# RMSNorm with swish on one core: one queue for x, and blocks of 8 rows instead of 4

## The chip, the cores and the metric

The kernel runs on one core of a Trainium2 chip. The metric is the device time of one execution in microseconds (us), the median over several runs. A profile is of one execution; its span is the time from the first to the last instruction that the profiler recorded.

Engines: DVE is VectorE, ACT is ScalarE, POOL is GpSimd, SP is SyncE (which here only issues transfers and waits). DMA means the core's 16 transfer engines. ACTq and SPq are the sequencers of ACT and SP, where transfers are issued. TensorE does nothing here.

## The reference

```python
batch, seq, dim = 16, 1024, 512          # x: float32, gamma: ones, eps: 1e-5

def reference(x, gamma, eps):
    rms = np.sqrt(np.mean(x ** 2, axis=-1, keepdims=True) + eps)
    x_norm = x / rms * gamma
    return (x_norm * (1.0 / (1.0 + np.exp(-x_norm)))).astype(np.float32)
```

x has 16384 rows of 512 floats, 33.55 MB; the output has the same size. So 67.1 MB must be moved. A row's result needs the sum of its squares, then `(mean + eps) ** -0.5`, a multiplication by this number and by gamma, and swish.

## The kernel before

Each of the 128 partitions owns 128 rows of x. They are cut into four groups of 32 rows per partition ("32 rows" always means 32 rows in each partition, 8.4 MB). The buffer `xb` holds 96 rows per partition: groups 0, 1 and 2 have places of their own, group 3 takes the place of group 0 (`slots`). Everything is done in place in `xb`, and the order of every engine's work is written out by hand with semaphores.

- Loads (`load`, L117) are issued by SP in the order of the list `loads`: 4, 4, 8, 16 and 32 rows of groups 0 and 1, then 28 + 4 rows of group 2 and 28 + 4 of group 3. Two are issued before the program's first barrier (`early`). A load whose place is still to be stored waits on SP for that store's landing (`st`).
- Stores (`store`, L191) are issued by ACT, in the middle of its stream of work: 28 + 4 rows of group 0, groups 1 and 2 whole, then 16 + 8 + 8 rows of group 3. Two of them are held back until a given load has landed (`hold`, L189), so that a store doesn't share the transfer engines with a load.
- Compute goes in chunks of `cn = 4` rows, 32 chunks. For chunk k, ACT squares: two rows go one at a time through an `activation` whose accumulator writes the row's mean of squares (L162, output to a `junk` tile), two rows are squared into a PSUM tile `sq` (L169), and DVE sums these (`sums`, L215). GpSimd adds eps (L143) and raises to the power -0.5 (L150). DVE multiplies each row by the result and gamma, one instruction a row (`norm`, L226). ACT applies swish to the 4 rows at once (`swish`, L181).
- The order on ACT is: squares of chunk k, stores that are due, swish of chunk k-2. The order on DVE is: sums of chunk k, multiplications of chunk k-1.
- At the start GpSimd clears three small tiles (L137 to L139), ACT loads gamma into four partitions (L199) and DVE spreads it (L239).

Of the kernel before, what the change touches and what calls it, by code (L numbers as in the profile page):

```python
# [9 lines left out]
def kernel(  # L10
# [7 lines left out]
    nc = tc.nc  # L18
    P = nc.NUM_PARTITIONS
    AF = mybir.ActivationFunctionType  # L20
    ALU = mybir.AluOpType
    fp32 = mybir.dt.float32

    xf = x.flatten_outer_dims()
    of = out.flatten_outer_dims()
    R, D = xf.shape

    groups = [32] * 4
    slots = [0, 32, 64, 0]
    loads = [(0, 0, 4), (0, 4, 4), (0, 8, 8), (0, 16, 16), (1, 0, 32)]  # L30
    loads += [(2, 0, 28), (2, 28, 4), (3, 0, 28), (3, 28, 4)]
    stores = [(0, 0, 28), (0, 28, 4), (1, 0, 32), (2, 0, 32)]
    stores += [(3, 0, 16), (3, 16, 8), (3, 24, 8)]
    hold = {0: (loads.index((2, 0, 28)), 12), 2: (loads.index((3, 0, 28)), 22)}
    behind = {}
    ring = 96
    early = 2
    cn = 4
    n_sq = 2

    first = [sum(groups[:g]) for g in range(len(groups))]
    assert P * sum(groups) == R, R
# [1 line left out]

    chunks = []
    for i, (g, r, n) in enumerate(loads):
        for c in range(r, r + n, cn):
            chunks.append((slots[g] + c, i if c == r else None))
    K = len(chunks)
    assert K * cn * P == R  # L50

    ends = [-(-(first[g] + r + n) // cn) for g, r, n in stores]

    inv_d = 1.0 / float(D)
    eps_f = float(eps)
# [4 lines left out]
    def sbuf(name, shape, dt=fp32):  # L60
        return nc.alloc_sbuf_tensor(name, shape, dt).ap()

    xb = sbuf("xb", [P, ring, D])
    gamma4 = sbuf("gamma4", [P, D])
    gamma_sb = sbuf("gamma_sb", [P, D])
    neg_half = sbuf("neg_half", [P, cn])
    ms = sbuf("ms", [P, K, cn])
    aeps = sbuf("aeps", [P, K, cn])
    rstd = sbuf("rstd", [P, K, cn])
    sq = [nc.alloc_psum_tensor(f"sq{i}", [P, n_sq, D], fp32).ap() for i in range(2)]  # L70
    junk = [nc.alloc_psum_tensor(f"junk{i}", [P, D], fp32).ap() for i in range(2)]

    ld = [nc.alloc_semaphore(f"ld{t}") for t in range(len(loads))]
    st = [nc.alloc_semaphore(f"st{t}") for t in range(len(stores))]
    scratch = nc.dram_tensor("scratch", [P, 16], fp32, kind="Internal").ap()
    blank = sbuf("blank", [P, 16])
    s_blank = nc.alloc_semaphore("s_blank")
    s_scratch = nc.alloc_semaphore("s_scratch")
    s_gld = nc.alloc_semaphore("s_gld")
    s_zero = nc.alloc_semaphore("s_zero")  # L80
    s_half = nc.alloc_semaphore("s_half")
    s_gamma = nc.alloc_semaphore("s_gamma")
    s_acc = nc.alloc_semaphore("s_acc")
    s_sq = nc.alloc_semaphore("s_sq")
    s_sum = nc.alloc_semaphore("s_sum")
    s_eps = nc.alloc_semaphore("s_eps")
    s_rstd = nc.alloc_semaphore("s_rstd")
    s_norm = nc.alloc_semaphore("s_norm")
    s_swish = nc.alloc_semaphore("s_swish")

    def need(ins, sem, value):
        return ins.wait_op(sem, value, "sem-ge")

    def dram(ap, piece):
        g, r, n = piece
        rows = ap[P * first[g] : P * (first[g] + groups[g])]
        return rows.rearrange("(p n) d -> p n d", n=groups[g])[:, r : r + n, :]

    def place(piece):
        g, r, n = piece  # L100
        return slots[g] + r, slots[g] + r + n

    def buf(piece):
        a, b = place(piece)
        return xb[:, a:b, :]

    stored_by_sync = set()

    def load(i):
        a, b = place(loads[i])  # L110
        for u, piece in enumerate(stores):
            c, d = place(piece)
            over = piece[0] < loads[i][0] and c < b and a < d
            if (over or behind.get(i) == u) and u not in stored_by_sync:
                nc.sync.wait_ge(st[u], 16)
                stored_by_sync.add(u)
        return nc.sync.dma_start(  # L117
            out=buf(loads[i]), in_=dram(xf, loads[i])
        ).then_inc(ld[i], 16)
# [3 lines left out]
    for t in range(early):  # L123
        ins = load(t).ins
        assert here[-1] is ins or here[-1].name == ins.name
        here.pop()
        at = next(
            i for i, other in enumerate(entry)
            if other.engine == mybir.EngineType.SP
            and isinstance(other, mybir.InstDrain)  # L130
        )
        entry.insert(at, ins)
    for t in range(early, len(loads)):
        load(t)
    nc.sync.wait_ge(s_scratch, 16)

    nc.gpsimd.memset(blank, 0.0).then_inc(s_blank, 1)  # L137
    nc.gpsimd.memset(gamma4, 0.0).then_inc(s_zero, 1)  # L138
    nc.gpsimd.memset(neg_half, -0.5).then_inc(s_half, 1)  # L139
    nc.gpsimd.wait_ge(s_half, 1)  # L140
    for k in range(K):
        need(
            nc.gpsimd.tensor_scalar(  # L143
                out=aeps[:, k, :], in0=ms[:, k, :], scalar1=eps_f, scalar2=None,
                op0=ALU.add,
            ),
            s_sum, k + 1,
        ).then_inc(s_eps, 1)
        need(
            nc.gpsimd.tensor_tensor(  # L150
                out=rstd[:, k, :], in0=aeps[:, k, :], in1=neg_half, op=ALU.pow
            ),
            s_eps, k + 1,
        ).then_inc(s_rstd, 1)

    def square(k):
        at, landing = chunks[k]
        if landing is not None:
            nc.scalar.wait_ge(ld[landing], 16)  # L159
        for j in range(n_sq, cn):  # L160
            n = k * (cn - n_sq) + j - n_sq
            acc = nc.scalar.activation(  # L162
                out=junk[n % 2], in_=xb[:, at + j, :], func=AF.Square,
                scale=inv_d**0.5, accum_out=ms[:, k, j : j + 1],
            )
            if n >= 2:
                need(acc, s_acc, n - 1)
            acc.then_inc(s_acc, 1)
        square = nc.scalar.activation(  # L169
            out=sq[k % 2], in_=xb[:, at : at + n_sq, :],  # L170
            func=AF.Square, scale=inv_d**0.5,
        )
        if k >= 2:
            need(square, s_sum, k - 1)
        square.then_inc(s_sq, 1)

    def swish(k):
        at, _ = chunks[k]
        rows = xb[:, at : at + cn, :]
        need(  # L180
            nc.scalar.activation(out=rows, in_=rows, func=AF.Silu), s_norm, k + 1  # L181
        ).then_inc(s_swish, 1)

    def after(t):
        return max((k for u, (_, k) in hold.items() if u <= t), default=0)

    def store(t):
        if t in hold:
            nc.scalar.wait_ge(ld[hold[t][0]], 16)  # L189
        need(  # L190
            nc.scalar.dma_start(out=dram(of, stores[t]), in_=buf(stores[t])),  # L191
            s_swish, ends[t],
        ).then_inc(st[t], 16)

    need(nc.scalar.dma_start(out=scratch, in_=blank), s_blank, 1).then_inc(
        s_scratch, 16
# [3 lines left out]
        s_zero, 1,  # L200
    ).then_inc(s_gld, 16)
    nc.scalar.preload_act_table_set("silu_and_others")  # L202
    stored = 0
    for k in range(K + 3):
        if k < K:
            square(k)
        while stored < len(stores) and max(ends[stored] + 2, after(stored)) <= k:
            store(stored)
            stored += 1
        if 2 <= k < K + 2:  # L210
            swish(k - 2)

    def sums(k):
        need(
            nc.vector.tensor_reduce(  # L215
                out=ms[:, k, 0:n_sq], in_=sq[k % 2], op=ALU.add,
                axis=mybir.AxisListType.X,
            ),
            s_sq, k + 1,
        ).then_inc(s_sum, 1)  # L220

    def norm(k):
        at, _ = chunks[k]
        for j in range(cn):
            row = xb[:, at + j, :]
            ins = nc.vector.scalar_tensor_tensor(  # L226
                out=row, in0=row, scalar=rstd[:, k, j : j + 1], in1=gamma_sb,
                op0=ALU.mult, op1=ALU.mult,
            )
            if j == 0:  # L230
                need(ins, s_rstd, k + 1)
        ins.then_inc(s_norm, 1)

    for k in range(K + 1):
        if k < K:
            sums(k)
        if k == 0:
            need(
                nc.vector.stream_shuffle(gamma_sb, gamma4, [0] * 32), s_gld, 16  # L239
            ).then_inc(s_gamma, 1)  # L240
        if k == 1:
            nc.vector.wait_ge(s_gamma, 1)
        if k >= 1:
            norm(k - 1)

    for t in range(len(stores)):
        if t not in stored_by_sync:
            nc.sync.wait_ge(st[t], 16)


# [33 lines left out]
```

## Time and profile before

| what | value |
|---|---|
| time, median of 3 runs | 161.33 us (159.96 to 161.42) |
| the profiled execution | 161.41 us, span 160.1 us |
| ACT busy | 129.7 us (81% of the span) |
| DVE busy | 124.4 us (78%) |
| POOL busy | 65.5 us (41%) |
| moved | 67.16 MB, mean 419 GB/s over the span |
| loads' queue (q1), stores' queue (q10) | 49.4% and 48.8% of the 16 transfer engines' time |

A row of the page's groups reads: line, engine, operation, output and inputs with their shapes, count, then the busy time in us and the mean of one in ns, then the idle time before them and what ended it. A row of the windows reads: stretch, its length, busy time of DVE, ACT and POOL in it (with counts), TensorE's clock, the mean busy share of the transfer engines, and GB/s. The share can be above 1 in a short stretch, since a packet is counted where it starts. The chain of waits is followed back from the last instruction of an engine; its pieces are given as start, length, and what was done.

### The profile page before, as it was taken

Reading aid. Unit: us, or ns where it says so; the run is one execution under the profiler, and the core shown is the slowest. Engines: PE = TensorE matmul, PEld = TensorE weight load, DVE = VectorE, ACT = ScalarE, POOL = GpSimd, SP = SyncE. Lnnn points to the kernel's source line nnn. Section 1 sums busy time; section 2 is a strip of 40 time slices with the busy share of each in tenths; the row PEclk is TensorE's granted clock in tenths of the full one; section 3 lists DMA queues with packets and bytes.
Section 4 is the critical chain, followed back from the end, with each engine's and each line's share of the span. In section 5 each row is a group of like instructions: output and inputs, shape, how many; then the busy total and the mean of one; then the engine's idle time right before and its main releaser. Section 6 shows DMA issues by size and latency. Waiting matters only on the chain.

```text
span 160.1 us, 496 instructions
## 1 busy us (share of the span) xinstructions
DVE 124.4 (78%) x162; ACT 129.7 (81%) x193; POOL 65.5 (41%) x71
## 2 busy tenths in 40 slices
DVE  0239989999199998899999999999999999970000
ACT  0937989994799988999999999999999999571000
POOL 1035555555055555555555555555555555500000
DMA  7999996996999997999969996996996997899896
GB/s 264 458 461 393 450 598 262 524 524 262 458 461 446 444 411 338 458 458 458 450 258 458 458 458 266 518 524 278 508 508 297 508 475 327 385 426 483 368 426 270
DMA packets 2460, 67.16 MB, mean 419 GB/s; under 512 B 404, under 2 KB 404, under 8 KB 408
## 3 DMA queue, kind: packets, MB, share of 16 engines
q1 hardware_dynamic: 1296, 33.56, 49.4%
q10 hardware_dynamic: 1160, 33.57, 48.8%
q14 instruction: 4, 0.03, 0.0%
HBM read 33.56 MB, written 33.56 MB: 419 GB/s over the span
## 4 chain that ended last, share of the span: by engine, by line
ACT 55%; DMA 24%; DVE 7%; issue 3%; ACTq 1%; SPq 0%
ACT xb L181 24%; DMA xb<-in_x_dram 24%; ACT junk L162 18%; ACT sq L169 13%; DVE xb L226 5%; DVE ms L215 2%; ACTq L191 1%; SPq L117 0%; ACTq L159 0%
## 5 line engine op out<-in xcount | busy, mean ns | idle before, releaser
L226 DVE SCALAR_TENSOR_TENSOR xb<-xb,rstd,gamma_sb 128x512 f32<-128x512 f32 x128 | 87.3, 744 | 0.0
L181 ACT ACTIVATE xb<-xb 128x2048 f32<-128x2048 f32 x32 | 60.9, 1902 | 4.8 <-DVE xb L226 3.8
L215 DVE TENSOR_REDUCE ms<-sq 128x2 f32<-128x1024 f32 x32 | 39.2, 1223 | 16.1 <-ACT sq L169 13.1
L143 POOL TENSOR_SCALAR aeps<-ms 128x4 f32<-128x4 f32 x32 | 20.6, 644 | 70.0 <-DVE ms L215 70.0
L150 POOL TENSOR_TENSOR rstd<-aeps,neg_half 128x4 f32<-128x4 f32 x32 | 44.0, 1376 | 2.7
L162 ACT ACTIVATE junk<-xb 128x512 f32<-128x512 f32 x64 | 37.2, 582 | 6.7 <-DMA xb<-in_x_dram 6.6
L169 ACT ACTIVATE sq<-xb 128x1024 f32<-128x1024 f32 x32 | 32.1, 1005 | 0.0
L162 ACT ACTIVATION_READ_ACCUMULATOR junk<-xb 128x1 f32 x64 | 11.9, 186 | 0.0
L202 ACT ACT_TABLE_LOAD x1 | 1.3, 1283 | 3.6 <-issue 3.6
L239 DVE LOAD_MASK_SELECT gamma_sb<-gamma x1 | 0.0, 14 | 2.5 <-DMA gamma<-in_gamma_dram 2.5
L239 DVE STREAM_SHUFFLE gamma_sb<-gamma 128x512 f32<-128x512 f32 x1 | 0.7, 715 | 0.0
L137 POOL MEMSET blank<- 128x16 f32 x1 | 0.1, 111 | 1.5 <-POOLq L58 1.5
L138 POOL MEMSET gamma<- 128x512 f32 x1 | 0.5, 525 | 0.0
L265 POOL MEMSET const-float32-0.0<- 128x1 f32 x1 | 0.1, 98 | 0.2 <-issue 0.2
L265 POOL MEMSET const-bfloat16-1.0<- 128x1 bf16 x1 | 0.1, 102 | 0.0
L265 POOL MEMSET const-uint8-127<- 128x1 uint8 x1 | 0.1, 101 | 0.0
L139 POOL MEMSET neg_half<- 128x4 f32 x1 | 0.1, 101 | 0.0
L265 POOL MEMSET const-float32-1.0<- 128x1 f32 x1 | 0.1, 98 | 0.0
## 6 DMA issues: line engine op xcount, KB each, us to landing
xb<-in_x_dram SPq DMA_DIRECT2D x2, 7168.0 KB, 38.4
out_dram<-xb ACTq DMA_DIRECT2D x1, 7168.0 KB, 19.3
xb<-in_x_dram SPq DMA_DIRECT2D x4, 1024.0 KB, 14.0
xb<-in_x_dram SPq DMA_DIRECT2D x1, 4096.0 KB, 19.5
out_dram<-xb ACTq DMA_DIRECT2D x1, 4096.0 KB, 20.1
out_dram<-xb ACTq DMA_DIRECT2D x2, 2048.0 KB, 16.1
xb<-in_x_dram SPq DMA_DIRECT2D x1, 2048.0 KB, 10.2
out_dram<-xb ACTq DMA_DIRECT2D x1, 1024.0 KB, 21.3
```

The source lines that it names most:

```text
L138: nc.gpsimd.memset(gamma4, 0.0).then_inc(s_zero, 1)
L143: nc.gpsimd.tensor_scalar(out=aeps[:, k, :], in0=ms[:, k, :], scalar1=eps_f, scalar2=None, op0=ALU.add,),
L150: nc.gpsimd.tensor_tensor(out=rstd[:, k, :], in0=aeps[:, k, :], in1=neg_half, op=ALU.pow),
L162: acc = nc.scalar.activation(out=junk[n % 2], in_=xb[:, at + j, :], func=AF.Square, scale=inv_d**0.5, accum_out=ms[:, k, j : j + 1],)
L169: square = nc.scalar.activation(out=sq[k % 2], in_=xb[:, at : at + n_sq, :], func=AF.Square, scale=inv_d**0.5,)
L181: nc.scalar.activation(out=rows, in_=rows, func=AF.Silu), s_norm, k + 1
L191: nc.scalar.dma_start(out=dram(of, stores[t]), in_=buf(stores[t])),
L202: nc.scalar.preload_act_table_set("silu_and_others")
L215: nc.vector.tensor_reduce(out=ms[:, k, 0:n_sq], in_=sq[k % 2], op=ALU.add, axis=mybir.AxisListType.X,),
L226: ins = nc.vector.scalar_tensor_tensor(out=row, in0=row, scalar=rstd[:, k, j : j + 1], in1=gamma_sb, op0=ALU.mult, op1=ALU.mult,)
L239: nc.vector.stream_shuffle(gamma_sb, gamma4, [0] * 32), s_gld, 16
L265: nc = _bacc.Bacc("TRN2", target_bir_lowering=False, num_devices=1)
```

## The change

SP issues the loads and the stores of x, all on its one queue, in a list `order`: loads of 8, 8, 16, 32 and 32 rows; stores of 24 and 8 rows of group 0; loads of 24 and 8 rows of group 3; then all other stores (groups 1 and 2, then 16 + 8 + 8 rows). A store waits on SP until swish has reached its last row. The holds are gone.

Compute goes in 16 blocks of 8 rows. Of these, 3 go through ACT's accumulator and 5 are squared into `sq` and summed by DVE. `sq` has two buffers of five rows; the first is in PSUM, the second now in SBUF. The addition of eps moves from GpSimd to DVE, right behind the sums, for all 8 rows; GpSimd does only the power, 16 times on 8 values instead of 32 times on 4. The three memsets move from GpSimd to DVE. Swish is one instruction for 8 rows, still two blocks behind the squares.

```diff
-    loads = [(0, 0, 4), (0, 4, 4), (0, 8, 8), (0, 16, 16), (1, 0, 32)]
-    loads += [(2, 0, 28), (2, 28, 4), (3, 0, 28), (3, 28, 4)]
-    stores = [(0, 0, 28), (0, 28, 4), (1, 0, 32), (2, 0, 32)]
+    loads = [(0, 0, 8), (0, 8, 8), (0, 16, 16), (1, 0, 32)]
+    loads += [(2, 0, 32), (3, 0, 24), (3, 24, 8)]
+    stores = [(0, 0, 24), (0, 24, 8), (1, 0, 32), (2, 0, 32)]
     stores += [(3, 0, 16), (3, 16, 8), (3, 24, 8)]
-    hold = {0: (loads.index((2, 0, 28)), 12), 2: (loads.index((3, 0, 28)), 22)}
+    turns = [(len(loads) - 2, 2)]
-    cn = 4
-    n_sq = 2
+    cn = 8
+    n_sq = {8: 5}
+    order = [("load", t) for t in range(early, turns[0][0])]
+    at = 0
+    for (i, u), (j, _) in zip(turns, turns[1:] + [(len(loads), 0)]):
+        order += [("store", t) for t in range(at, u)] + [("load", t) for t in range(i, j)]
+        at = u
+    order += [("store", t) for t in range(at, len(stores))]
...
-    sq = [nc.alloc_psum_tensor(f"sq{i}", [P, n_sq, D], fp32).ap() for i in range(2)]
+    sq = [
+        nc.alloc_psum_tensor("sq0", [P, n_max, D], fp32).ap(),
+        sbuf("sq1", [P, n_max, D]),
+    ]
...
-    for t in range(early, len(loads)):
-        load(t)
+    for kind, t in order:
+        if kind == "load":
+            load(t)
+        else:
+            need(
+                nc.sync.dma_start(out=dram(of, stores[t]), in_=buf(stores[t])),
+                s_swish, ends[t],
+            ).then_inc(st[t], 16)
...
-    nc.gpsimd.memset(blank, 0.0).then_inc(s_blank, 1)
-    nc.gpsimd.memset(gamma4, 0.0).then_inc(s_zero, 1)
-    nc.gpsimd.memset(neg_half, -0.5).then_inc(s_half, 1)
-    nc.gpsimd.wait_ge(s_half, 1)
-    for k in range(K):
-        need(
-            nc.gpsimd.tensor_scalar(
-                out=aeps[:, k, :], in0=ms[:, k, :], scalar1=eps_f, scalar2=None,
-                op0=ALU.add,
-            ),
-            s_sum, k + 1,
-        ).then_inc(s_eps, 1)
+    for k, (_, row, n, _) in enumerate(chunks):
         need(
             nc.gpsimd.tensor_tensor(
-                out=rstd[:, k, :], in0=aeps[:, k, :], in1=neg_half, op=ALU.pow
+                out=rstd[:, row : row + n], in0=ms[:, row : row + n],
+                in1=neg_half[:, :n], op=ALU.pow,
             ),
             s_eps, k + 1,
         ).then_inc(s_rstd, 1)
...
-    for k in range(K + 3):
+    for k in range(K + 2):
         if k < K:
             square(k)
-        while stored < len(stores) and max(ends[stored] + 2, after(stored)) <= k:
-            store(stored)
-            stored += 1
-        if 2 <= k < K + 2:
+        if k >= 2:
             swish(k - 2)
 
+    nc.vector.memset(blank, 0.0).then_inc(s_blank, 1)
+    nc.vector.memset(gamma4, 0.0).then_inc(s_zero, 1)
+    nc.vector.memset(neg_half, -0.5)
+
     def sums(k):
+        _, row, n, _ = chunks[k]
         need(
             nc.vector.tensor_reduce(
-                out=ms[:, k, 0:n_sq], in_=sq[k % 2], op=ALU.add,
-                axis=mybir.AxisListType.X,
+                out=ms[:, row : row + n_sq[n]], in_=sq[k % 2][:, : n_sq[n], :],
+                op=ALU.add, axis=mybir.AxisListType.X,
             ),
             s_sq, k + 1,
         ).then_inc(s_sum, 1)
+        need(
+            nc.vector.tensor_scalar(
+                out=ms[:, row : row + n], in0=ms[:, row : row + n],
+                scalar1=eps_f, scalar2=None, op0=ALU.add,
+            ),
+            s_sum, k + 1,
+        ).then_inc(s_eps, 1)
```

## The prediction

> **What bounds the kernel now.** I read the page first: engines, queues and chain.
>
> ```profile
> DVE 124.4 (78%) x162; ACT 129.7 (81%) x193; POOL 65.5 (41%) x71
> q1 hardware_dynamic: 1296, 33.56, 49.4%
> q10 hardware_dynamic: 1160, 33.57, 48.8%
> ACT 55%; DMA 24%; DVE 7%; issue 3%; ACTq 1%; SPq 0%
> ```
>
> The two transfer queues together fill 98.2% of the 16 transfer engines' time. The chain names ACT, but it is followed back from the last store, so it shows only why that store was issued when it was. The windows and the last store's landing (the view of `out_dram`, from 143 us on) show what ends the run:
>
> ```profile
> 145.00:160.00 15.00, 0.00 (x0) 0.00 (x0) 0.00 (x0) 1.00 0.91 387
> L191 ACTq DMA_DIRECT2D out_dram<-xb x1: 339/339/339, 144.9 to 144.9; - x1
> DMA to landing us min/median/max: 15.2/15.2/15.2
> ```
>
> All engines are done at 144.9 us, and the stores queued behind each other take 15 us more. Now the two 32-row stores before them, same view, other windows:
>
> ```profile
> L191 ACTq DMA_DIRECT2D out_dram<-xb x1: 338/338/338, 99.6 to 99.6; - x1
> DMA to landing us min/median/max: 21.8/21.8/21.8
> ...
> L191 ACTq DMA_DIRECT2D out_dram<-xb x1: 339/339/339, 114.3 to 114.3; - x1
> DMA to landing us min/median/max: 26.4/26.4/26.4
> ```
>
> Group 1's store lands at 99.6 + 21.8 = 121.4 and group 2's at 114.3 + 26.4 = 140.7, 19.3 us later. The other three land at 150.3, 155.2 and 160.1. So 32 rows cost 19.3 us of transfer, 16 rows 9.65, 8 rows 4.85, and everything after group 1's store takes 38.7 us. Group 2's store was issued 7.1 us before group 1's had landed. That lead is the number to watch: the transfers bound the kernel, compute is second, and its slack at that place is about 7 us, at the end 10 us (144.9 against 155.2).
>
> The compute pace, first from the page's groups:
>
> ```profile
> L226 DVE SCALAR_TENSOR_TENSOR xb<-xb,rstd,gamma_sb 128x512 f32<-128x512 f32 x128 | 87.3, 744 | 0.0
> L181 ACT ACTIVATE xb<-xb 128x2048 f32<-128x2048 f32 x32 | 60.9, 1902 | 4.8 <-DVE xb L226 3.8
> L215 DVE TENSOR_REDUCE ms<-sq 128x2 f32<-128x1024 f32 x32 | 39.2, 1223 | 16.1 <-ACT sq L169 13.1
> L143 POOL TENSOR_SCALAR aeps<-ms 128x4 f32<-128x4 f32 x32 | 20.6, 644 | 70.0 <-DVE ms L215 70.0
> L150 POOL TENSOR_TENSOR rstd<-aeps,neg_half 128x4 f32<-128x4 f32 x32 | 44.0, 1376 | 2.7
> L162 ACT ACTIVATE junk<-xb 128x512 f32<-128x512 f32 x64 | 37.2, 582 | 6.7 <-DMA xb<-in_x_dram 6.6
> L169 ACT ACTIVATE sq<-xb 128x1024 f32<-128x1024 f32 x32 | 32.1, 1005 | 0.0
> ```
>
> And two rows of the timeline, a stretch without waits on DVE (start, length, instruction):
>
> ```profile
> 136.40 1.23 DVE L215 TENSOR_REDUCE ms<-sq 128x2 f32<-128x1024 f32 x1
> 137.54 5.38 DVE L226 SCALAR_TENSOR_TENSOR xb<-xb,rstd,gamma_sb 128x512 f32<-128x512 f32 x8
> ```
>
> Eight multiplies take 5.38, so one every (5.38 - 0.744) / 7 = 0.662 us; the one behind a reduce starts 1.14 after it, 0.09 before its end. Back to back, DVE needs 2 x 1.14 + 8 x 0.662 = 7.58 us for 8 rows. ACT, in the chain, repeats 1.23 + 0.91 + 1.87 = 4.01 for 4 rows, 8.02 for 8. ACT sets the pace, with DVE close behind.
>
> **The change, part by part.**
>
> *Rows shift from ACT to DVE.* A block of 8 rows has 3 rows summed by ACT's accumulator and 5 by DVE's reduce; before it was 4 and 4.
> ACT per block: 3 accumulates at 1.23 / 2 = 0.615 give 1.84. The five-row square: one more 512 elements costs 1.005 - 0.581 = 0.424, so 1.005 + 3 x 0.424 = 2.28 (bounds 2.28 and, in proportion, 2.51). The eight-row swish: 1.90 + 4 x 0.424 = 3.60 (at most 3.80). Sum 7.7, less some 0.1 of overlap: ACT gains 0.4.
> DVE per block: the reduce of five rows isn't in the trace. A further row costs at least (1223 - 744) ns = 0.48 (reduce less a one-row multiply) and at most 1223 / 2 = 0.61. So it takes 2.66 to 3.06. The shuffle, like the reduce a one-source pass, is the nearest row: 715 ns for 512 elements, so 0.51 a row. I take 0.52 and 2.78. The add of eps on DVE is new. Lower bound nothing (hidden), upper 0.66 (GpSimd's median for this operation); I take a multiply without its elements, 0.744 - 0.53, about 0.20. It waits for its own reduce's semaphore: 0.04, as between a square's end and its reduce's start. Sum: 2.78 + 0.04 + 0.20 - 0.08 overlap + 8 x 0.662 = **8.24 us per block** (bounds 7.88 and 8.98). DVE becomes the bound, slower per row than ACT was.
>
> A rule that speaks against this change: the Trainium skill, page "VectorE: DVE Perf Modes", section "The perf-mode tier table (the rule you actually need)", gives `tensor_reduce` only the single-rate mode, in SBUF as in PSUM, so the SBUF half of the square buffer brings no rate. With the page's 0.96 GHz clock (section "Specifications") a row is 512 / 0.96 = 533 ns, an estimate from the page; the reduce would take 2.82, the block 8.28, and the end come 0.4 us later.
>
> *Blocks of 8 instead of 4.* Swish still comes two blocks behind the squares, so it trails by 16 rows instead of 8. At about 1 us a row this makes every store ready some 8 us later; it was 7.1 us early.
>
> *All of x on SP's queue.* ACT loses seven issues (0.34 to 1.05 us each; 1.0 us of idle before a swish at 60.5 is theirs). ACT no longer bounds, so this brings nothing. Order of SP: 96 rows of loads, stores of 24 and 8 rows, loads of 24 and 8, then the rest. Store 0 waits for swish 2 (about 49 us) and store 1 for swish 3 (about 57), both before the loads have landed. The load of 24 rows waits for store 0's landing; store 1, 4.85 us long, covers its start. In the kernel before, the last 32 rows of loads ran from store 1's landing at 80.7 to 101.9, 21.2 us instead of 19.3, so the fixed order saves 1.9. Transfers alone: 61.3 (the last load of the first 96 rows, issued at 3.9 and 57.4 under way) + 14.5 + 4.85 + 14.5 + 4.85 + 19.3 = 119.3 for group 1's store, + 38.7 = 158.0.
>
> *Covered edits.* GpSimd loses 32 adds and half the powers; DVE waits for a power only if it exceeds the eight multiplies between (5.3 us against 1.38; if uncovered, 1.4 per block). The memsets go to DVE, which idled until 7.2; gamma landed at 10.9 and is needed near 19. Without cover: 0.6 once.
>
> **The path that sets the end.** The load of group 1 lands at 41.14 as before (same bytes ahead of it):
>
> ```profile
> 2.75 38.38 DMA xb<-in_x_dram
> ```
>
> ACT begins at 41.22; block 4's squares take 1.84 + 2.28, and its reduce starts at 45.38. DVE is free by then: block 1's reduce starts at about 16.3 (load at 12.1, squares 4.1), three blocks of 8.24 and one wait of 1.4 for block 2's squares give 42.5. From 45.38 DVE runs without a pause, since ACT needs 7.6. Block 13's reduce starts at 45.38 + 9 x 8.24 = 119.5, which is when block 11's multiplies end (119.6). Swish 11: 3.60, to 123.2. Store 3 (group 2) is issued at 123.3, but SP's queue has been empty since 119.3. **That is the new wait.** A transfer into an idle queue: the first load, issued at 0.0, moves nothing for about 1.0 (the window 0 to 2 us has a share of 0.49), and its 4 rows land at 4.6, 2.2 more than their 2.4 of transfer. So 1.0 to 2.2; I take 1.2, since the start of the program burdens the larger one. End: 123.3 + 1.2 + 38.7 = 163.2. What follows has slack: store 4 is ready at about 140 (needed 144), store 5 at 148 (154), store 6 at 153.5 (158).
>
> The profiled execution took 161.41 with a span of 160.1, so 1.3 lie around it; the median of the runs is 161.33, 0.1 less. 163.2 + 1.3 - 0.1 = **164.4 us**, 1.9% above before.
>
> **Rivals.**
> A, faster: the queue never runs empty and the end is 158.0, 159.2 us in all. Store 3 must be issued by 119.3 - 1.2 = 118.1, so 9 blocks must fit in 118.1 - 3.7 - 45.4 = 69.0: 7.67 a block. For it: transfers fill 98% of the span. Against it: eight multiplies leave 2.4 for reduce and add, below even the lower bound of 2.66 for the reduce less its 0.08.
> B, no change: reduce at its lower bound, the add nearly hidden. 7.88 to 8.05 a block moves the end by 9 x (-0.36 to -0.19): 161.2 to 162.7.
> C, slower still: the add on DVE is as dear as on GpSimd. 0.66 instead of 0.20 makes the block 8.70, store 3 4.1 us later: 168.5. For it: GpSimd's median is 0.66. Against it: the shortest one there, at 8.5 us while DVE was idle, took 0.23, so 0.66 is not the price of the add itself.
>
> A second rule against the change stands by itself: the Trainium skill, "SBUF — State Buffer", section "Who interferes with whom", lets a two-port instruction such as the add wait until a GpSimd instruction has finished. No row of this trace has a blocked one; a whole power (1.38) would be 12 us over nine blocks, but the last power began a block's multiplies earlier and is over.
>
> **Numbers.** Forecast 0.66, A 0.12, B 0.14, C 0.08. Its own range is 163.1 to 166.3 (block 8.1 to 8.45). Left out may be A (0.12) and most of C (0.07), so the range takes in B and the lower edge of C: 161.2 to 167.2. About 1% can be told from no change here; so faster 0.12, same 0.14, slower 0.74.
>
> **What would show it.** DVE without idle time from about 45 to 150 us, ACT waiting for DVE before each swish; a block period of 8.1 to 8.45; store 3 issued near 123 and the transfer share near nothing for some 5 us from 119; the loads all landed near 100 instead of 102; the last multiplies near 150, the last swish near 153.5. If the reduce of five rows takes under 2.4 or the transfers run without a hole, the forecast is wrong.

## The result, and the profile after

The changed kernel takes 165.04 us (median of 4 runs, 164.93 to 165.18), against 160.82 us for the kernel before in the runs beside it (159.96 to 161.42). The ratio is 1.0267, 95% interval 1.0209 to 1.0324: slower, as forecast, at 164.4 us in a range of 161.2 to 167.2. The profiled execution took 164.93 us with a span of 163.6, so again 1.3 us lie around the span.

The page of the changed kernel (engines, loads' and stores' queue in one, and the chain):

```profile
DVE 132.8 (81%) x165; ACT 124.2 (76%) x129; POOL 32.9 (20%) x20
q1 hardware_dynamic: 2016, 67.11, 96.3%
DVE 64%; DMA 24%; ACT 5%; issue 0%; SPq 0%; ACTq 0%
```

ACT and DVE have changed places: DVE is now the busier engine, and the chain runs over DVE where it ran over ACT. All 67.11 MB went through one queue, at 96.3% of the transfer engines' span instead of 98.2%. The groups, with the rows that the forecast had to estimate:

```profile
L240 DVE SCALAR_TENSOR_TENSOR xb<-xb,rstd,gamma_sb 128x512 f32<-128x512 f32 x128 | 86.1, 746 | 0.0
L198 ACT ACTIVATE xb<-xb 128x4096 f32<-128x4096 f32 x16 | 57.8, 3615 | 13.5 <-DVE xb L240 13.5
L222 DVE TENSOR_REDUCE ms<-sq 128x5 f32<-128x2560 f32 x16 | 45.1, 2819 | 14.2 <-ACT sq L186 14.2
L163 POOL TENSOR_TENSOR rstd<-ms,neg_half 128x8 f32<-128x8 f32 x16 | 32.7, 2044 | 108.0 <-DVE ms L229 108.0
L186 ACT ACTIVATE sq<-xb 128x2560 f32<-128x2560 f32 x16 | 36.9, 2304 | 0.0
L229 DVE TENSOR_SCALAR ms<-ms 128x8 f32<-128x8 f32 x16 | 2.8, 172 | 0.5
```

The reduce of five rows takes 2.82 us, the add 0.17, the eight-row swish 3.62 and the five-row square 2.30. One block in the chain of waits (start, length, piece):

```profile
111.35 2.75 DVE ms L222
114.09 0.02 issue
114.12 0.17 DVE ms L229
114.29 5.29 DVE xb L240 x8
119.58 2.74 DVE ms L222
```

119.58 - 111.35 = 8.23 us per block; DVE's only pause in it is 0.02 us between the reduce and the add that waits for it. Then the stores (view of `out_dram`, windows around 90 and 123 us: group 1's store, group 2's) and the windows there (the columns after the length are DVE, ACT and POOL busy, TensorE's clock, transfer share, GB/s):

```profile
L156 SPq DMA_DIRECT2D out_dram<-xb x1: 344/344/344, 90.3 to 90.3; - x1
DMA to landing us min/median/max: 32.0/32.0/32.0
...
L156 SPq DMA_DIRECT2D out_dram<-xb x1: 344/344/344, 123.3 to 123.3; - x1
DMA to landing us min/median/max: 20.8/20.8/20.8
```

```profile
116.00:119.00 3.00, 3.00 (x6) 3.00 (x5) 0.44 (x1) 1.00 0.86 371
119.00:122.00 3.00, 3.00 (x2) 2.45 (x2) 0.00 (x0) 1.00 0.05 22
122.00:124.00 2.00, 1.97 (x5) 2.00 (x4) 1.40 (x1) 1.00 0.00 0
```

Here is the new wait. From 119 to 124 us the transfer engines move almost nothing, while DVE works without a break: group 2's store is issued at 123.3. From there to the end of the span it is 163.6 - 123.3 = 40.3 us of transfers. All 16 transfer engines end together, between 163.4 and 163.6 (the trace has a landing for each of them).

One thing doesn't fit the forecast. Group 1's store landed at 90.3 + 32.0 = 122.3, not at 119.3. A transfer lands when the last of the 16 engines is done, and in the trace's landings fourteen engines were done between 119.3 and 120.2, the other two at 121.6 and 122.3. The kernel before has such a lag too, but a smaller one: there fourteen engines were done with group 1's store between 120.2 and 120.4, the other two at 121.3. So for the slowest engine the empty stretch was short, and the question for the experiments was whether DVE or the one queue had cost the time.

### The profile page after: what moved, and what is told of

Its sections match the earlier page's. It is cut to its first block, busy times and chain, and to the rows that moved or that the text cites. A ratio compares the mean times of both kernels' runs of the same rounds, so it can differ in the third digit from the quotient of the medians.

```text
span 163.6 us, 377 instructions
## 1 busy us (share of the span) xinstructions
DVE 132.8 (81%) x165; ACT 124.2 (76%) x129; POOL 32.9 (20%) x20
## 3 DMA queue, kind: packets, MB, share of 16 engines
q1 hardware_dynamic: 2016, 67.11, 96.3%
## 4 chain that ended last, share of the span: by engine, by line
DVE 64%; DMA 24%; ACT 5%; issue 0%; SPq 0%; ACTq 0%
DVE xb L240 42%; DMA xb<-in_x_dram 24%; DVE ms L222 20%; ACT xb L198 2%; ACT sq L186 1%; DVE ms L229 1%; ACT junk L178 1%; SPq L135 0%; ACTq L176 0%
## 5 line engine op out<-in xcount | busy, mean ns | idle before, releaser
L240 DVE SCALAR_TENSOR_TENSOR xb<-xb,rstd,gamma_sb 128x512 f32<-128x512 f32 x128 | 86.1, 746 | 0.0
L198 ACT ACTIVATE xb<-xb 128x4096 f32<-128x4096 f32 x16 | 57.8, 3615 | 13.5 <-DVE xb L240 13.5
L222 DVE TENSOR_REDUCE ms<-sq 128x5 f32<-128x2560 f32 x16 | 45.1, 2819 | 14.2 <-ACT sq L186 14.2
L163 POOL TENSOR_TENSOR rstd<-ms,neg_half 128x8 f32<-128x8 f32 x16 | 32.7, 2044 | 108.0 <-DVE ms L229 108.0
L178 ACT ACTIVATE junk<-xb 128x512 f32<-128x512 f32 x48 | 28.0, 583 | 11.7 <-DMA xb<-in_x_dram 11.7
L186 ACT ACTIVATE sq<-xb 128x2560 f32<-128x2560 f32 x16 | 36.9, 2304 | 0.0
L178 ACT ACTIVATION_READ_ACCUMULATOR junk<-xb 128x1 f32 x48 | 9.0, 187 | 0.0
L229 DVE TENSOR_SCALAR ms<-ms 128x8 f32<-128x8 f32 x16 | 2.8, 172 | 0.5
L216 DVE MEMSET gamma<- 128x512 f32 x1 | 0.5, 485 | 0.1
```

The lines of the kernel that those rows point to most:

```text
L163: nc.gpsimd.tensor_tensor(out=rstd[:, row : row + n], in0=ms[:, row : row + n], in1=neg_half[:, :n], op=ALU.pow,),
L178: acc = nc.scalar.activation(out=junk[n_acc % 2], in_=xb[:, at + j, :], func=AF.Square, scale=inv_d**0.5, accum_out=ms[:, row + j : row + ...
L186: square = nc.scalar.activation(out=sq[k % 2][:, : n_sq[n], :], in_=xb[:, at : at + n_sq[n], :], func=AF.Square, scale=inv_d**0.5,)
L198: nc.scalar.activation(out=block, in_=block, func=AF.Silu), s_norm, k + 1
L216: nc.vector.memset(gamma4, 0.0).then_inc(s_zero, 1)
L222: nc.vector.tensor_reduce(out=ms[:, row : row + n_sq[n]], in_=sq[k % 2][:, : n_sq[n], :], op=ALU.add, axis=mybir.AxisListType.X,),
```

## The experiments

All times are medians beside the kernel before, which took 159.8 to 159.9 us (median) in these runs. Two theories stood at the start. *The empty queue*: block 11 is late, and the issue of group 2's store sets the end. *The lagging queue*: one queue for loads and stores makes some transfer engines fall behind, and the end can't come earlier whatever compute does.

**Group 2's store in two halves**, compute unchanged:

```diff
-    stores = [(0, 0, 24), (0, 24, 8), (1, 0, 32), (2, 0, 32)]
+    stores = [(0, 0, 24), (0, 24, 8), (1, 0, 32), (2, 0, 16), (2, 16, 16)]
```

> Only the store of group 2 is cut into 16 + 16 rows; compute is that of the changed kernel. Theory (SP's queue runs empty because block 11 is late): the first half needs only block 9 (ready near 106.8), the second is issued at 123.3 while the first still moves, so no hole near 119 to 124. The end is then set by the last store (issued at 153.3, + 1.2 + 4.85 = 159.3): span 159.3, 160.6 us, 4.4 us below the changed kernel. Rival (the one queue itself lags: in the changed kernel the slowest transfer engine landed group 1's store at 122.3, 3 us behind the first): the hole was covered by that lag, the span can't fall below 122.3 + 38.7 = 161.0, so 162.3 us.

Measured: 162.21 us (162.03 to 162.69), ratio 1.0130 (1.0082 to 1.0179), span 160.8. The hole at 119 to 124 is filled, and another has opened. Windows of this kernel:

```profile
119.00:124.00 5.00, 4.97 (x6) 4.45 (x5) 1.35 (x1) 1.00 1.03 446
138.00:139.00 1.00, 0.97 (x3) 1.00 (x1) 0.00 (x0) 1.00 0.08 33
139.00:140.00 1.00, 1.00 (x3) 0.75 (x1) 0.89 (x1) 1.00 0.08 33
140.00:141.00 1.00, 1.00 (x3) 0.00 (x0) 1.00 (x1) 1.00 1.22 524
```

The share of 0.08 at 138 to 140 us is one or two of 16 engines still working (1/16 is 0.06); the others wait for the next late store, 16 rows of group 3, issued at 139.8. The theory named the last store as the next limit and overlooked this one, so the run is 1.6 us above it. It shows that the late store was worth 2.8 us (165.04 to 162.21), but not what remains: one lagging engine was done with group 2 only at 141.3, and with the 19.3 us for the last 32 rows it would have ended near 160.6 without a second hole too. The rival's 162.3 was met, so this run doesn't decide between the two.

**Four rows through the reduce instead of five:**

```diff
-    n_sq = {8: 5}
+    n_sq = {8: 4}
```

> 4 of 8 rows through DVE's reduce instead of 5, all else as in the changed kernel. Theory (DVE's block time sets the issue of group 2's store): a row less is 0.53 us on DVE, 7.70 a block; ACT has 0.2 more, about 7.8, and sets the pace. Group 2's store at 119.6 instead of 123.3, span 159.9, 161.3 us. Rival (one queue lags): not below 162.3 us.

Measured: 162.34 us (161.50 to 162.84), ratio 1.0129 (1.0072 to 1.0185), span 161.3; group 2's store was issued at 119.8. In the landings fifteen engines ended between 159.85 and 160.05, which is the span that the first theory gave, and one at 161.2, which is the other's. Both were right, each for its engines; the metric takes the slowest.

**The add of eps back on GpSimd** (the `tensor_scalar` moves from `nc.vector` to `nc.gpsimd`, ahead of the power):

> The add of eps goes back to GpSimd, 16 adds of 8 values; all else as in the changed kernel. Theory: DVE's block loses 0.25 (0.17 for the add, 0.08 of lost overlap and wait), 7.98 instead of 8.23; nine blocks bring group 2's store to 121.0 and the span to 161.3, 162.7 us. Rival (one queue lags): 162.3 us or more, so no less; the time of issue of group 2's store tells whether the block's price is right.

Measured: 163.17 us (163.08 to 163.29), ratio 1.0185 (1.0130 to 1.0240), span 161.9, group 2's store issued at 121.5. The block in the chain takes 117.87 - 109.84 = 8.03 us, 0.20 less and not 0.25. The chain has the reduce (L229 in this kernel) and the multiplies back to back:

```profile
109.84 2.74 DVE ms L229
112.58 5.30 DVE xb L240 x8
117.87 2.73 DVE ms L229
```

Store and end move together: 1.8 us earlier (123.3 to 121.5), 1.9 us faster (165.04 to 163.17).

**The queue alone.** Compute of the kernel before (chunks of 4 rows, eps on GpSimd); loads, stores and SP's order of the changed kernel:

```diff
-            store(stored)                      # on ACT, held behind loads
+    for kind, t in [("load", 2), ("load", 3), ("load", 4), ("store", 0), ("store", 1),
+                    ("load", 5), ("load", 6)] + [("store", u) for u in range(2, len(stores))]:
+        ...                                    # all issued by nc.sync
```

> Compute of the kernel before (chunks of 4 rows, eps on GpSimd), with the loads, stores and the one SP queue of the changed kernel. Theory (the queue is not what slows): group 2's store is ready near 112, the queue never empties, transfers alone take to 158.0: span 158.0 to 158.5, 159.5 us, 1.5 us below before. Rival (one queue lags): span 161.0 or more, 162.3 us, slower than before.

Measured: 162.29 us (161.66 to 162.69), ratio 1.0127 (1.0075 to 1.0180), span 161.4. The forecast's own view of the queue falls here: with no store late, the one queue is slower than the two, not faster. Its last store and last windows:

```profile
L138 SPq DMA_DIRECT2D out_dram<-xb x1: 332/332/332, 143.9 to 143.9; - x1
DMA to landing us min/median/max: 17.4/17.4/17.4
```

```profile
158.00:159.00 1.00, 0.00 (x0) 0.00 (x0) 0.00 (x0) 1.00 0.12 49
159.00:160.00 1.00, 0.00 (x0) 0.00 (x0) 0.00 (x0) 1.00 0.08 33
160.00:161.00 1.00, 0.00 (x0) 0.00 (x0) 0.00 (x0) 1.00 0.04 16
```

A share of 0.12 is about two of 16 engines, 0.04 less than one: from 158 us on only one or two are at work. Fourteen engines had ended by 158.8, near the 158.0 of the sum; the last two took until 159.9 and 161.3. In the packets, each engine's last load packet ahead of the first store took 3.0 to 4.2 us instead of 2.4 (3.2 to 4.2 in the changed kernel), so the turn, the place in the order where loads are followed by stores, was the suspect. In the texts below a ring is the queue of one issuing engine: q1 for SP, q10 for ACT.

**Small loads ahead of the stores**, to see whether the size of that packet matters, on top of the queue alone:

```diff
-    loads += [(2, 0, 32), (3, 0, 24), (3, 24, 8)]
+    loads += [(2, 0, 28), (2, 28, 4), (3, 0, 24), (3, 24, 4), (3, 28, 4)]
...
```

(SP's order of issue is changed to match the list.)

> As the run with the queue alone (compute of the kernel before, all of x on SP's queue), but the loads right ahead of a store are 4 rows (28 + 4, and 24 + 4 + 4), so the last packet of a load on each transfer engine is 8 KB instead of 64 or 16 KB. In the run with the queue alone every engine's last 64 KB packet ahead of the first store took 3.2 to 4.2 us instead of 2.4, and the two slowest engines ended at 161.3 and 159.9 while the other fourteen ended at 158.1 to 158.8. Theory (the turn from loads to stores on one ring holds up the packet that is under way, in proportion to its size): the hold-up shrinks to 0.1 to 0.3 us, span 159.3 to 160.0, 160.6 to 161.3 us. Rival (a turn costs its 1.1 us whatever the packet, or the lag has nothing to do with turns): span 161 or more, 162.3 us again.

Measured: 161.95 us (160.78 to 162.72), ratio 1.0108 (1.0058 to 1.0159). That is within the scatter of the run before it and above the first theory's range: no gain from the small packet is seen.

**More turns**, group 0 stored and group 3 loaded in pieces of 8 rows in turn:

```diff
-    loads += [(2, 0, 32), (3, 0, 24), (3, 24, 8)]
-    stores = [(0, 0, 24), (0, 24, 8), (1, 0, 32), (2, 0, 32)]
+    loads += [(2, 0, 32), (3, 0, 8), (3, 8, 8), (3, 16, 8), (3, 24, 8)]
+    stores = [(0, 0, 8), (0, 8, 8), (0, 16, 8), (0, 24, 8), (1, 0, 32), (2, 0, 32)]
...
```

(SP's order of issue is again changed to match the lists.)

> As the run with the queue alone, but group 0 is stored and group 3 loaded in pieces of 8 rows in turn, so there are four turns from loads to stores instead of two, the extra two with 16 KB packets. Theory (each turn costs): at the turn with 16 KB packets the run with the queue alone lost 0.3 on most engines and 1.3 on the slowest; two more give a span of 161.9 to 164, 163.2 to 165.3 us. Rival (no cost of turns): 161.3, 162.3 us as before.

Measured: 164.68 us (164.41 to 165.23), ratio 1.0289 (1.0242 to 1.0335). Two more turns cost 164.68 - 162.29 = 2.4 us. In the landings the first engine to end does so 1.9 us later than with two turns (160.0 against 158.1) and the last one 2.0 us later (163.4 against 161.3). But this is no even price of 1 us a turn. By the earliest landing of each piece, the alternating pieces of 8 rows took 4.5 to 5.3 us, about the 4.85 of any 8 rows; most of the loss came at the last turn, where the 8 rows ahead of group 1's store took 6.5 us, against 5.2 in the run with two turns. By the latest landing, the 8 rows ahead of the second turn took 6.2 and those ahead of the last one 6.7, while the third turn cost nothing (4.9). Pieces are smaller here too, so it is the alternation as a whole that was priced.

**The changed kernel with the small loads**, compute unchanged:

> The changed kernel with the same small loads ahead of the stores; compute unchanged. Theory (group 2's store, issued at 123.3, sets its end, and the empty stretch before covers the lag): span 163.6, 165.0 us, no change, though the transfers ahead of the empty stretch end earlier on the slowest engine. Rival (the lag adds to the end of the changed kernel): 1 to 2 us less.

Measured: 164.97 us (164.95 to 165.00), ratio 1.0303 (1.0258 to 1.0347). No change: its group 2 store is issued at 123.3 and lands 20.8 us later, to the tenth as in the changed kernel. The small loads had not cured the lag here either (group 1's store landed at 90.4 + 32.3 = 122.7), so this run shows only that the smaller loads do nothing for the end, and not that the lag is free in the changed kernel.

**Both mended**: four rows through the reduce, group 2's store in halves, small loads:

> The changed kernel with 4 of 8 rows through DVE's reduce, group 2's store in two halves, and the small loads ahead of the stores. Theory (two causes, late stores and turns): no empty stretch, since the halves are ready near 104 and 120 and the 16 rows of group 3 near 135; the end is that of the run with the queue alone and small turns: span 159.3 to 160.0, 160.6 to 161.3 us, level with the kernel before. Rival (turns cost the same whatever the packets): span 161.2, 162.4 us.

Measured: 162.53 us (161.00 to 163.00), ratio 1.0134 (1.0087 to 1.0181). No store was late, and the time is that of the queue alone, as the rival said. Its profiled execution was the fastest of the six (161.0) and is not typical.

**Two rings.** As the run with the small loads on the queue alone, but ACT issues the stores on its own queue, held as in the kernel before:

```diff
-    hold = {0: (loads.index((2, 0, 28)), 12), 2: (loads.index((3, 0, 28)), 22)}
+    hold = {0: (loads.index((2, 0, 28)), 12), 2: (loads.index((3, 24, 4)), 22)}
```

(the rest of the kernel before stands, with the load and store lists of the run with the small loads)

> As the run with the queue alone and small turns (compute of the kernel before, loads ending in 4 rows ahead of a store), but the stores are issued by ACT on its own queue, held as in the kernel before until the load in front has landed. Only the ring of the stores and their hold differ. Theory (a turn from loads to stores within one ring holds up the slowest engine by 1.3 to 1.8 us, a turn across rings doesn't): group 1's store follows the last load on the slowest engine without loss, span 158.5 to 160, 159.6 to 161.2 us, level with the kernel before and some 2 us below the run with small turns (161.95). Rival (the pieces of 24 + 8 rows, not the ring, make the difference): 161.9 again.

Measured: 160.61 us (160.07 to 161.63), ratio 1.0046 (1.0018 to 1.0074). That is 1.3 us less than with the same pieces on one ring; the two intervals still touch, and the trace is clearer. The two 28 + 4 row loads ahead of the first store, issued at 2.8 and 3.2 or 3.3 us, show the turn in one line each (minimum is the first load's time to landing, maximum the second's). One ring:

```profile
L116 SPq DMA_DIRECT2D xb<-in_x_dram x2: 436/543/650, 2.8 to 3.2; - x2
DMA to landing us min/median/max: 56.2/58.1/59.9
```

Two rings:

```profile
L117 SPq DMA_DIRECT2D xb<-in_x_dram x2: 483/535/587, 2.8 to 3.3; - x2
DMA to landing us min/median/max: 56.2/57.2/58.2
```

With the store behind it in the same ring, the 4 rows land at 3.2 + 59.9 = 63.1, 4.1 us after the load in front (59.0); with the store in the other ring, at 61.5, 2.5 after it, the plain transfer time of 4 rows. Two things differ, though: the ring, and the hold, by which ACT issues a store behind loads only when all but the last 4 rows in front have landed, while SP issues it long before. One ring with a hold, or two rings without one, was not run, so which of the two saves the time is not shown.

**Swapped rings**: loads of groups 0 to 2 on SP, stores of group 0 and loads of group 3 on ACT's queue, all later stores on SP's:

> Compute of the kernel before; the ring changes at each turn from loads to stores and stays at the turn from stores to loads: loads of groups 0 to 2 on SP, stores of group 0 and loads of group 3 on ACT's queue, all later stores on SP's, waiting for the last load but one. Theory: loads to stores across rings is free, as in the kernel before, and stores to loads within a ring is free, as in the run with the queue alone (the slowest engine moved 24 rows in 14.5 us behind the store there, while the kernel before lost 1.9 at that place). Span 158.0 to 158.8, 159.3 to 160.1 us, at or just below the kernel before. Rival (each turn costs about 1 us wherever it is): 160.5 us or more.

Measured: 160.35 us (159.82 to 161.88), ratio 1.0036 (1.0000 to 1.0071). That lies between the two forecasts, level with the two rings and at most 0.7% above the kernel before; its profiled execution had a span of 158.9, but the median isn't below before. The first store behind a turn waits for a load's landing here as well, so this run doesn't separate ring and hold either. No version that was run beats the kernel before.

## Why the prediction was right, and where it was not

*The DVE block* carried the forecast and held: 8.24 us forecast, 8.23 measured. The reduce was 2.82 instead of 2.78, the add 0.17 instead of 0.20, the gap between them 0.02 instead of 0.04. These misses, +0.04, -0.03 and -0.02, nearly cancel, so that the sum agrees to 0.01 is in part luck. The estimate by the Trainium skill, page "VectorE: DVE Perf Modes", sections "The perf-mode tier table (the rule you actually need)" (single rate for `tensor_reduce`) and "Specifications" (0.96 GHz), was 2.82, and 2.82 was measured. The trace agrees with the rule for the SBUF half too: all 16 reduces, eight from PSUM and eight from SBUF, lie between 2.81 and 2.83.

*The path to group 2's store*: issue at 123.3, measured 123.3. *From there to the end*: 1.2 + 38.7 = 39.9 forecast, 40.3 measured. The start into the empty queue took 1.5 instead of 1.2 (20.8 from issue to landing, less 19.3 of transfer). Together that is 163.2 against 163.6 of span, 0.4 of the 0.64 us between 164.4 and 165.04; the rest is that the median lies 0.1 above the profiled execution, where the forecast put it 0.1 below, and rounding.

*Blocks of 8 instead of 4* were said to make every store ready some 8 us later. The run with four rows through the reduce shows this part nearly alone: its chain repeats in 7.86 us a block, about the old pace (8.02 for 8 rows), and group 2's store is issued at 119.8; with chunks of 4 rows, in the run with the queue alone, it was issued at 113.4. That is 6.4 us of lead.

*The size against before* was too small (1.9% against 2.67%), because the sum was set against a profiled execution and a median of three (161.41, 161.33) from the upper part of what the kernel before does: in the later runs its median was 159.8.

*The wrong step* is the one on SP's queue. It credited the fixed order with 1.9 us and gave "transfers alone" as 158.0, and rival A was built on it. Measured with no store late, the one queue ends at 161.4, behind the kernel before. The step took the loss of 1.9 us at the turn from stores to loads, which a single ring does remove (the 24 rows behind the store landed in 14.5 us on the slowest engine), and overlooked that the single ring loses time at its turns from loads to stores. In the changed kernel the last load of the first 96 rows landed at 63.0 instead of 61.3, and the 8 rows ahead of group 1's store took 5.95 instead of 4.85; that is most of the 3 us between 119.3 and 122.3. In the kernel before these turns go from one ring to the other, behind a hold. The step also took one landing time for all engines, while one or two of 16 fall behind; its 119.3 was right for the fastest of them. The sign that the loads would all have landed near 100 failed with it: the last engine was done at 103.0.

This error hardly showed in the forecast time, which was luck: the two causes overlap instead of adding up. While the fourteen faster engines wait for the late store, the two slow ones catch up, and in the changed kernel all engines end within 0.2 us (163.4 to 163.6). Without the late store the time would still be about 162.3 (162.21, 162.29 and 162.53 in three runs), not 159.2. So of the 5.2 us above the 159.8 of the later runs, about half goes with the late store and about half stays with the one queue.

*Covered edits*: the power of 8 values took 2.04 us, more than the 1.38 that was taken over from 4 values, and is covered by the 5.3 of the multiplies, as the prediction had it; POOL still waited for DVE for 108.0 us.

What stays open: why an engine loses time at a turn when the stores stand right behind the loads in one ring, whether the ring or the missing hold does it, and why the same turn costs one or two of the 16 engines more. The kernel with the changed compute and two rings was not run.

## What to carry to other kernels

In a kernel whose transfers never pause, look for the store with the smallest lead over the queue and follow the slower compute to that place; the shares of busy time, and the last store, said nothing of it. Coarser blocks cost every store some of its lead (6.4 us here at about equal pace), whatever they save in instructions. When a transfer's landing is compared with bytes over rate, look at the slowest of the engines, and before loads and stores are put on one queue, look at the turns from loads to stores.

## What was not expected of the hardware

- Where stores stand right behind loads in one queue, the loads ahead of the turn slow down: with the queue alone, the first 96 rows had landed at 60.9 to 61.4 us on fourteen transfer engines and at 63.2 on the slowest, against 60.2 to 60.5 and 61.4 in the kernel before. At the second turn the 8 rows ahead took 5.2 us by the earliest landings and 6.2 by the latest, instead of 4.85. With 8 KB packets in place of 64 KB at the first turn the time hardly moved (161.95, 162.29).
- Moving group 2's store by 1.8 us moved the end by 1.9: the queue had run empty, and passed the late issue on one to one.
- GpSimd's power took 1.38 us for 4 values a partition and 2.04 for 8, so half as many instructions saved a quarter of its time (44.0 to 32.7 us).
